# Hybrid decoder layer with a PEER mixer: 24 instead of 16 tokens take their U products from gathered rows, and two of eight heads of the fourth token block are searched later

## The chip, the core and the metric

The kernel runs on one core of a Trainium2 chip, whose engines are named as in the profile: PE (TensorE), DVE (VectorE), ACT (ScalarE), POOL (GpSimd) and SP (SyncE, which here only sets off DMAs). The metric is the device time of one execution in microseconds. Before the change it is 1616.67 us, the median of three runs (1615.92 to 1617.07).

## The reference, cut to what matters

One layer for 512 tokens of width 1024 in float32: a mixer of state-space heads and latent attention (not touched by the change), and then PEER, a lookup among 16384 experts:

```
def block(xb):                                   # 128 tokens at a time
    q = (xb @ w_query).reshape(T, 8, 2, 128)     # 8 heads, two halves
    s = jnp.einsum('thkd,hknd->thkn', q, sub_keys)           # 128 sub-keys a half
    sv, si = lax.top_k(s, 16)                    # best 16 of each half
    cand_s = sv[:, :, 0, :, None] + sv[:, :, 1, None, :]     # 256 candidates a head
    cand_i = si[:, :, 0, :, None] * 128 + si[:, :, 1, None, :]
    top_s, top_pos = lax.top_k(cand_s, 16)       # 16 experts a head
    expert_idx = jnp.take_along_axis(cand_i, top_pos, axis=-1)
    gate = jax.nn.softmax(top_s, axis=-1)
    u = jnp.take(u_table, expert_idx, axis=0)    # rows of a 16384 x 1024 table
    act = jax.nn.gelu(jnp.einsum('td,thkd->thk', xb, u), approximate=False)
    v = jnp.take(v_table, expert_idx, axis=0)
    return jnp.einsum('thk,thkd->td', gate * act, v)
```

So each token has 128 pairs of an expert and a gate (8 heads by 16). A residual sum and a layer norm follow.

## The kernel before

**Arithmetic.** Nearly all products are float32 made of three products of a split form: a weight tile `wir` is read from memory, ScalarE rounds it to its high part `wih` (L109), VectorE subtracts to get the low part `wil` (L119), and `mm3` (L71 to L74) multiplies high by high, high by low and low by high. The class `Stream` holds the weights in one fixed order (`item()` gives the next). Fetching an item also has the splits made of the two items behind it and the raw loads of those after, which SP issues; so the low part of a U item is made, in VectorE's order, about two U chunks before TensorE needs it. During the query products the low part is GpSimd's (`lo_on`).

**PEER in two ways.** Blocks 0 to 2 of the tokens (`NT` = 384) are computed against the whole tables: a *U chunk* (`u_half`, L1223) multiplies 128 experts' rows of the U table by the transposed tokens, 8 x 3 matmuls whose moving side is `NU` tokens wide, and a Gelu (L1233) leaves `act`. A *V chunk* (`v_mm`, L1385) multiplies `act` times gate by 128 rows of the V table, 18 matmuls of 512 columns into six banks that are summed over all 128 chunks. The gate times activation is made in `v_prep` (P, L1362), and split by `v_hi` (Ph, ScalarE L1375) and `v_lo` (Pl, VectorE L1382). Block 3 is done by gathering rows: 128 rows of U for its 128 tokens, products on VectorE (L1440), and 128 rows of V (L1446), each by an indirect DMA of GpSimd (L1429, five buffers).

**The last `UG` tokens of block 2** are not in the U chunks (`NU` = `NT` - `UG`). For each of them its 128 expert rows are gathered (`ug_index` L1057, `ug_fetch` L1069, three buffers `urow`), multiplied by the token's row spread over the partitions (`ux`) and summed by one VectorE instruction (`ug_dots`, L1078). Those activations are multiplied into the gate (`ug_head`, L1088), and the chunks' `act` is filled with ones there (L1232), with a scale per token.

**Stages around the change** (us in the profile of before):

- 423 to 549: query products `w_query_fm`, sub-key scores, and the search on VectorE. `top16` (L947) runs max, max_index, match_replace, max, max_index for each of the four token blocks; `stage1` (L964) does so for both halves of a head and then for 88 sums that hold its best 16.
- 549 to 593: `stage2` (L1037) decodes the indices of blocks 0 to 2; those of block 3 are stored to memory and decoded much later (`late3`, L1044).
- 595 to 770: the *build*. `build_g` (L1126) makes the gate matrix, 128 x 128 experts for every token of blocks 0 to 2, in 48 groups of eight tokens. `hot` makes two one-hot tiles on VectorE (ij L1134, g L1139), one group ahead; TensorE does 16 small float16 matmuls (L1157, L1158); ScalarE copies them to `stg` (L1160); every fourth group its queue stores them in two parts (gs0 L1164, gsp L1165). From group 1 on, one product of `ug_dots` follows each group.
- 770 to 790: the rest of the first `LEAD` = 54 U chunks and, behind the first gate loads (`load_g`, L1333, issued by SP, L1337), the first V chunk.
- 790 to 1382: one U chunk and one V chunk in turns. The gather of block 3 is mixed in by `gather` (L1407), which begins with `late3`.
- 1382 to 1606: V chunks alone.

**What sets the order.** The order on each engine is written out. Two clocks of estimated time are kept, `tm[0]` for TensorE and `tm[1]` for VectorE; `drive` (L1278) puts the next half U chunk (`T_U`/2 us) when TensorE's is behind, and else the next piece of the stage's generator, whose `yield` tells its cost. In search, decode and build, U chunks are so put until `LEAD` - `RES` = 52 of them are placed. Each group of the build adds 2.42 us, each product 1.2. In the V stage, `pump` (L1176) takes pieces of `gather` worth 2.1 us for a V chunk and twice that where a U chunk goes with it, until the rows begin; from there the share of the rows that is due is worked out from the units left.

Of the kernel before, what the change touches and what calls it, by code (L numbers as in the profile page):

```python
# [11 lines left out]
F32 = mybir.dt.float32  # L12
# [12 lines left out]
D = 1024  # L25
NB = 4
# [14 lines left out]
ENDU = 15  # L41
# [12 lines left out]
def tile_block(ctx: ExitStack, tc: tile.TileContext, I, out):  # L54
# [11 lines left out]
    def close(*ps):  # L66
        for p in ps:
            opened.remove(p)
            p.release()
# [810 lines left out]
    one = xt.tile([128, UG], F32, name="one")  # L880
    scl = xt.tile([128, 1], F32, name="scl")
    V.memset(one, 1.0)
    V.memset(scl, 1.0)
# [33 lines left out]
            V.tensor_tensor(ol, pv_, oh, op=OP.subtract)  # L917

    sc, qT = {}, {}

    def w_query_fm(m):
        if m < 16:
# [24 lines left out]
    def top16(src, w, val, idx):  # L947
        t2 = []
        for b in range(NB):
            V.max(val[:, b, 0:8], src[:, b])  # L950
        for b in range(NB):
            V.max_index(idx[:, b, 0:8], val[:, b, 0:8], src[:, b])
        for b in range(NB):
            t2.append(rt.tile([128, 128], F32, name="t2", bufs=4)[:, :w])
            V.match_replace(t2[b], val[:, b, 0:8], src[:, b], NEG)  # L955
        for b in range(NB):
            V.max(val[:, b, 8:16], t2[b])
        for b in range(NB):
            V.max_index(idx[:, b, 8:16], val[:, b, 8:16], t2[b])
        return NB * (0.36 + w * 0.0064)  # L960

    IJG = {}

    def stage1(m):  # L964
        yield top16(sc.pop(m), 128, TV4[:, :, m], TI4[:, :, m])
        if m % 2:
            h = m // 2
            cand = rt.tile([128, NB, 88], F32, name="cand")
            for c0, a0, na, w in ((0, 0, 1, 16), (16, 1, 3, 8), (40, 4, 12, 4)):
                sh = [128, NB, na, w]  # L970
                V.tensor_tensor(cand[:, :, c0:c0 + na * w].rearrange("p h (a b) -> p h a b", a=na),
                                TV4[:, :, m - 1, a0:a0 + na, None].to_broadcast(sh),
                                TV4[:, :, m, None, 0:w].to_broadcast(sh), op=OP.add)
            yield 0.7 + top16(cand, 88, TS4[:, :, h], PO4[:, :, h])

    t3d = [dram.tile([128, n, 16], dt, name=nm) for n, dt, nm in ((8, F32, "ts3"), (8, U32, "po3"), (16, U32, "ti3"))]

    def decode(p, TS, PO, TI, ia, blocks, nb):
        f4 = lambda z: z.rearrange("p b h k -> p (b h k)")
# [56 lines left out]

    def stage2():  # L1037
        for dst, t in zip(t3d, (TS4, PO4, TI4)):
            nc.sync.dma_start(dst, t[:, 3])
        yield from decode(rt2, TS4[:, :3], PO4[:, :3], TI4[:, :3], iaE, (0, 1, 2), 3)  # L1040

    late = []
# [12 lines left out]
    GT, UR = {}, {}  # L1055

    def ug_index(tmp):  # L1057
# [6 lines left out]
        G.dma_start(UR["ix"], bass.AP(tensor=ugi.tensor, offset=ugi.offset, ap=[[UG, 128 // UG], [128, UG], [1, UG]]))  # L1064
        G.dma_start(UR["g"], ugg)
        for n in range(3):
            ug_fetch(n)

    def ug_fetch(n):  # L1069
        if n < UG:  # L1070
            UR[n] = ug.tile([128, D], F32, name="urow", bufs=3)
            G.indirect_dma_start(out=UR[n], out_offset=None, in_=I["u"],
                                 in_offset=bass.IndirectOffsetOnAxis(ap=UR["ix"][:, n:n + 1], axis=0))

    def ug_dots():
        for n in range(UG):
            r = UR.pop(n)
            V.scalar_tensor_tensor(r, r, 1.0, UR["x"], op0=OP.mult, op1=OP.mult, accum_out=UR["hd"][:, n:n + 1])  # L1078
            ug_fetch(n + 3)
            yield 1.2  # L1080
        A.activation(UR["hd"], UR["hd"], AF.Gelu)
        G.dma_start(bass.AP(tensor=ugh.tensor, offset=ugh.offset, ap=[[UG, 128 // UG], [128, UG], [1, UG]]), UR["hd"])
        G.dma_start(UR["w"], ugh)
        close(ug)
        aps.append(pool("act2"))
        yield 0.1
# [39 lines left out]
    def build_g():  # L1126
# [19 lines left out]
        for n in range(48):  # L1146
# [15 lines left out]
            tm[0] += 0.95  # L1162
            if g % 4 == 3:
                nc.scalar.dma_start(gs0[b * 4 + g // 4], stg[:, 0:8])  # L1164
# [58 lines left out]
    def u_half(c, e, psum=None):  # L1223
# [68 lines left out]
    for m in range(17):  # L1292
# [9 lines left out]
        while tm[1] < tm[0] + T_Q:  # L1302
            c = next(fill, None)
            if c is None:
# [4 lines left out]
    close(rq)  # L1309
    ug = pool("ug")  # L1310
    UR["x"] = ug.tile([128, D], F32, name="ux")
    nc.sync.dma_start(UR["x"], bass.AP(tensor=xsp.tensor, offset=xsp.offset + (3 * 128 - UG) * D,
                                       ap=[[0, 128 // UG], [D, UG], [1, D]]))
    UR["ix"] = ijp.tile([128, UG], I32, name="uix")
# [11 lines left out]
    UR["w"] = gb.tile([UG, 128], F32, name="uw")  # L1326
    UR["m"] = gb.tile([UG, 2], F32, name="um")
    drive(build_g(), 1)
    close(gb, *gs)
    vst = pool("vst")  # L1330
    gt = {}

    def load_g(q):  # L1333
        if q < 32 and q not in gt:
            gt[q] = vst.tile([128, NT // 32, 4, 32], F32, name="gt", bufs=2)
            src, q0 = (gs0, q * 4) if q < 2 else (gsp, q * 4 - 8)
            nc.sync.dma_start(gt[q], src[:, :, q0:q0 + 4, :].rearrange("b j i t -> j b i t"))  # L1337

    for q in range(2):
        load_g(q)  # L1340
    if UO:
        step_u()
    uc = un[0]
# [128 lines left out]
    while vc <= LASTC:  # L1472
# [166 lines left out]
```

## Time and profile before

| | |
|---|---|
| median of three runs | 1616.67 us (1615.92 to 1617.07) |
| the profiled execution | 1618.11 us, with a span of 1616.4 us from the first to the last instruction |
| granted TensorE clock | 0.997 on average |
| moved by DMA | 395.42 MB in 152253 packets, 245 GB/s on average |
| 423 to 549 us, search | PE busy 125.8 us, DVE 117.9, 110 GB/s |
| 549 to 595 us, decoding | PE 44.9, DVE 43.8, 171 GB/s |
| 595 to 770 us, build | PE 173.8, DVE 169.1, 269 GB/s |
| 790 to 1382 us, U and V | PE 592.0, DVE 499.3, 340 GB/s |
| 1382 to 1606 us, V alone | PE 224.0, DVE 196.1, 297 GB/s |

Each row of the stages adds up the time in which an engine ran an instruction. Where PE's busy time is the length of the stretch, TensorE never waited there; how dense its matmuls are inside has to be seen in single instructions, since a busy matmul includes its pipeline's length. The rows that matter are shown below with the argument.

### The profile page before, as it was taken

The numbers are of one execution on the slowest core, as the hardware profiler recorded it, in microseconds if no ns is written. First come the engines' busy times: TensorE is split into PE (matmuls) and PEld (weight loads), VectorE is DVE, ScalarE is ACT, GpSimd is POOL, SyncE is SP. The second block draws the span as 40 slices with busy tenths as digits, with TensorE's granted clock in tenths as the row PEclk, the third lists the DMA queues.
The fourth block names the chain that finished last, engine by engine and source line by source line (L and its number), as shares of the span: only waits on it lengthen the run. The fifth ranks groups of instructions, "written<-read, shape, count | busy, mean of one in ns | idle before, by whom it ended". The sixth has DMA issues, their size and how long they took to land.

```text
span 1616.4 us, 23785 instructions
## 1 busy us (share of the span) xinstructions
PE 1581.7 (98%) x8643; PEld 1392.5 (86%) x8643; DVE 1357.5 (84%) x2564; ACT 708.9 (44%) x1231; POOL 479.2 (30%) x340
## 2 busy tenths in 40 slices
PE   6999999999999999999999999999999999999997
PEld 5787878878888999999999999999999999888886
DVE  8979767746799999999488888888888888989987
ACT  5575467732433445556443433333333333333341
POOL 0000010000133223100045555555555555555300
PEclk9999999999999999999999999999999999999999
DMA  6242122364333458877689999999999999999963
GB/s 242 96 156 88 52 77 55 107 234 156 121 91 93 126 173 324 295 250 251 215 293 363 347 357 352 352 346 341 350 351 354 342 346 360 351 336 365 333 226 120
DMA packets 152253, 395.42 MB, mean 245 GB/s; under 512 B 12776, under 2 KB 65720, under 8 KB 150344
## 3 DMA queue, kind: packets, MB, share of 16 engines
q1 hardware_dynamic: 104952, 213.19, 39.6%
q0 software_dynamic: 43584, 155.29, 26.2%
q10 hardware_dynamic: 3600, 25.43, 4.1%
q8 instruction: 68, 1.11, 0.3%
q14 instruction: 49, 0.40, 0.1%
HBM read 359.99 MB, written 31.78 MB: 242 GB/s over the span
## 4 chain that ended last, share of the span: by engine, by line
PE 80%; DVE 14%; ACT 3%; DMA 1%; issue 1%; DVEq 0%; ACTq 0%
PE va L1391 10%; PE va L1395 10%; PE va L1392 10%; PE pu L72 10%; PE pu L74 10%; PE pu L73 10%; PE pa L74 3%; PE pa L73 3%; PE pa L72 3%; DVE t L955 1%; PE pw L73 1%; PE pw L74 1%; PE pw L72 1%; PE pw L1157 1%; DVE wil L119 1%; PE pw L1158 1%
## 5 line engine op out<-in xcount | busy, mean ns | idle before, releaser
L109 ACT ACTIVATE wih<-wir 128x1024 fp32r<-128x1024 f32 (+2 forms) x269 | 278.0, 1034 | 300.2 <-DMA wir<-ut 108.1
L119 DVE TENSOR_TENSOR wil<-wir,wih 128x1024 fp32r<-128x1024 f32 (+1 forms) x254 | 302.0, 1190 | 94.0 <-ACT wih L109 54.8
L74 PE MATMUL pu<-XTH,wil 128*128 128x368 f32 x1008 | 331.8, 329 | 1.0 <-DVE wil L119 0.9
L72 PE MATMUL pu<-XTH,wih 128*128 128x368 f32 x904 | 299.9, 332 | 0.1
L73 PE MATMUL pu<-XTL,wih 128*128 128x368 f32 x904 | 296.8, 328 | 0.0
L1392 PE MATMUL va<-wil,Ph 128*128 128x512 f32 x726 | 282.7, 389 | 0.0
L1429 POOL DMA_INDIRECT row<-u,ix x128 | 191.3, 1494 | 245.1 <-DVE row L1440 122.9
L1429 POOL DMA_INDIRECT row<-v,ix x128 | 189.2, 1478 | 173.1 <-DVE ac L1446 147.8
L74 PEld LDWEIGHTS pu<-XTH,wil 128*128 128x128 f32 x1008 | 189.0, 188 | 1.8 <-DVE wil L119 1.6
L72 PEld LDWEIGHTS pu<-XTH,wih 128*128 128x128 f32 x904 | 169.5, 188 | 3.2 <-ACT act L1233 0.3
L73 PEld LDWEIGHTS pu<-XTL,wih 128*128 128x128 f32 x904 | 169.7, 188 | 2.9
L1391 PE MATMUL va<-wih,Ph 128*128 128x512 f32 x432 | 168.5, 390 | 0.0
L1446 DVE SCALAR_TENSOR_TENSOR ac<-row,hd,ac 128x1024 f32<-128x1024 f32 x128 | 164.1, 1282 | 3.5 <-DMA row<-v,ix 1.3
L1392 PEld LDWEIGHTS va<-wil,Ph 128*128 128x128 f32 x726 | 136.2, 188 | 26.0
L1440 DVE SCALAR_TENSOR_TENSOR row<-row,x 128x1024 f32<-128x1024 f32 x128 | 150.5, 1220 | 4.3 <-DMA row<-u,ix 4.3
L109 ACT ACTIVATE wihx<-wir 128x1024 fp32r<-128x1024 f32 x67 | 71.1, 1061 | 156.8 <-DMA wir<-v 141.5
L1395 PE MATMUL va<-wih,Pl 128*128 128x512 f32 x432 | 133.3, 390 | 0.0
L1233 ACT ACTIVATE act<-pu 128x368 f32<-128x368 f32 x126 | 59.7, 474 | 163.2 <-PE pu L74 163.1
L1391 PE MATMUL va<-wihx,Ph 128*128 128x512 f32 x294 | 114.8, 391 | 0.0
L119 DVE TENSOR_TENSOR wil<-wir,wihx 128x1024 fp32r<-128x1024 f32 x62 | 75.8, 1223 | 41.3 <-issue 29.9
L1395 PEld LDWEIGHTS va<-wih,Pl 128*128 128x128 f32 x432 | 81.2, 188 | 17.2
L1391 PEld LDWEIGHTS va<-wih,Ph 128*128 128x128 f32 x432 | 81.1, 188 | 15.8
(458 smaller groups left out, 3073.4 us busy)
## 6 DMA issues: line engine op xcount, KB each, us to landing
wir<-ut SPq DMA_DIRECT2D x128, 512.0 KB, 5.7
wir<-v SPq DMA_DIRECT2D x128, 512.0 KB, 6.6
gsp<-stg ACTq DMA_DIRECT2D x12, 1920.0 KB, 7.9
gt<-gsp SPq DMA_DIRECT2D x30, 768.0 KB, 10.5
wir<-wo SPq DMA_DIRECT2D x26, 512.0 KB, 3.7
wir<-wf SPq DMA_DIRECT2D x18, 512.0 KB, 3.4
wir<-wqr SPq DMA_DIRECT2D x16, 512.0 KB, 3.7
de<-acd POOLq DMA_DIRECT2D x8, 512.0 KB, 5.1
```

The costliest lines, as they stand in the source:

```text
L72: T.matmul(ps, lh, rh, start=start, stop=False)
L73: T.matmul(ps, lh, rl, start=False, stop=False)
L74: T.matmul(ps, ll, rh, start=False, stop=stop)
L109: A.activation(h, r, AF.Copy)
L119: self.lo(n).tensor_tensor(l, r, h, op=OP.subtract)
L1233: A.activation(ACT[c][:, :NU], ps, AF.Gelu)
L1391: T.matmul(va[b][e], Ph[:, bs], h[:, cs], start=c == 0, stop=False)
L1392: T.matmul(va[b][e], Ph[:, bs], l[:, cs], start=False, stop=False)
L1395: T.matmul(va[b][e], Pl[:, bs], h[:, cs], start=False, stop=c == 127)
L1429: G.indirect_dma_start(out=R[s], out_offset=None, in_=I["u"] if s < 128 else I["v"], in_offset=bass.IndirectOffsetOnAxis(ap=ix[:, s % 128: ...
L1440: V.scalar_tensor_tensor(r, r, 1.0, x3, op0=OP.mult, op1=OP.mult, accum_out=hd[:, s:s + 1])
L1446: V.scalar_tensor_tensor(ac, r, hd[:, s - 128:s - 127], ac, op0=OP.mult, op1=OP.add)
```

## The change

1. `UG` goes from 16 to 24. The U chunks' moving side shrinks from 368 to 360 tokens, and 24 tokens are gathered, in two index tiles of 16 and 8 (`UGS`). Two products follow each group of the build where one did, so that they end at group 13 and not at group 16. The spread token rows hold 16 tokens at a time (each spread over eight partitions); the tile `ux` is loaded again, by GpSimd, ahead of product 16.
2. The search over block 3 leaves out heads 6 and 7 (score tiles 12 to 15, `LM` = 12): ScalarE's queue stores their scores of block 3 to memory (`sc3`), and `late3` reads them back and searches them in the V stage, ahead of block 3's decoding.
3. The last store of the gate (gsp of group 47) is taken from ScalarE's queue and put on SP's, behind the first two gate loads. The gate tiles `gt` get a pool of their own, opened before the build's buffers are closed, so that these loads don't depend on that store.
4. Planner constants: `T_U` from 4.07 to 4.0, and `pump`'s share in front of the rows from 2.1 to 2.2.

The core of the diff:

```diff
-UG = 16
+UG = 24
+LM = 12
+UGS = ((16, 8), (8, 0))
...
-T_U = 4.07
+T_U = 4.0
...
         A.activation(sc[m].rearrange("p a b -> p (a b)"), ps, AF.Copy)
+        if m >= LM:
+            nc.scalar.dma_start(sc3d[:, m - LM], sc[m][:, 3])
...
     def stage1(m):
-        yield top16(sc.pop(m), 128, TV4[:, :, m], TI4[:, :, m])
+        nb = NB if m < LM else 3
+        z = lambda t, k: t[:, :nb, k]
+        yield top16(rt, sc.pop(m)[:, :nb], 128, z(TV4, m), z(TI4, m))
         if m % 2:
...
+            yield head_top(rt, z(TV4, m - 1), z(TV4, m), z(TS4, m // 2), z(PO4, m // 2))
...
     def late3():
...
+        s3 = lt.tile([128, 1, 16 - LM, 128], F32, name="sc3")
+        nc.sync.dma_start(s3[:, 0], sc3d)
         for z, src in zip(t, t3d):
-            nc.sync.dma_start(z[:, 0], src)
+            nc.sync.dma_start(z[:, 0, :src.shape[1]], src)
+        tv = lt.tile([128, 1, 16 - LM, 16], F32, name="tv")
         yield 3.4
+        for m in range(LM, 16):
+            yield top16(lt, s3[:, :, m - LM], 128, tv[:, :, m - LM], t[2][:, :, m])
+            if m % 2:
+                yield head_top(lt, tv[:, :, m - LM - 1], tv[:, :, m - LM], t[0][:, :, m // 2], t[1][:, :, m // 2])
         yield from decode(lt, *t, ia, (3,), 1)
...
+    def ug_x(q, c, o):
+        UR["x"] = ug.tile([128, D], F32, name="ux")
+        q.dma_start(UR["x"], bass.AP(tensor=xsp.tensor, offset=xsp.offset + (3 * 128 - UG + o) * D,
+                                     ap=[[0, 128 // c], [D, c], [1, D]]))
...
     def ug_dots():
         for n in range(UG):
+            if n == 16:
+                ug_x(G, *UGS[1])
+                yield 0.0
+                yield 0.0
             r = UR.pop(n)
...
             if g % 4 == 3:
                 nc.scalar.dma_start(gs0[b * 4 + g // 4], stg[:, 0:8])
-                nc.scalar.dma_start(gsp[b * 4 + g // 4], stg[:, 8:])
+                if n < 47:
+                    nc.scalar.dma_start(gsp[b * 4 + g // 4], stg[:, 8:])
+                else:
+                    GT["last"] = stg
...
             if n >= 1:
-                tm[1] += next(dots, 0.0)
+                for _ in range(2):
+                    tm[1] += next(dots, 0.0)
...
-            A.activation(ACT[c][:, NU:], one, AF.Copy)
+            A.activation(ACT[c][:, NU:], one[:, 0:1].to_broadcast([128, UG]), AF.Copy)
...
     drive(build_g(), 1)
-    close(gb, *gs)
-    vst = pool("vst")
+    close(gb)
+    gtp = pool("gtp")
...
     for q in range(2):
         load_g(q)
+    nc.sync.dma_start(gsp[11], GT.pop("last")[:, 8:])
+    close(*gs)
+    vst = pool("vst")
...
         if GS[0] < 0:
-            more = pump(fill, 2.1 * w)
+            more = pump(fill, 2.2 * w)
```

`head_top` holds the 88 sums and their `top16`, which stood in `stage1`; `top16` runs over as many blocks as its source has. `stage2` stores the indices of heads 0 to 5 of block 3 only.

More of the change, by code (lines that the diff above doesn't have):

```diff
@@ L879, in tile_block @@
     XTL = xt.tile([128, 8, S], F32R, name="XTL")
-    one = xt.tile([128, UG], F32, name="one")
+    one = xt.tile([128, 16], F32, name="one")
     scl = xt.tile([128, 1], F32, name="scl")
@@ L919, in tile_block @@
     sc, qT = {}, {}
+    sc3d = dram.tile([128, 16 - LM, 128], F32, name="sc3")
     def w_query_fm(m):
@@ L945, in sub_scores, with top16 @@
         A.activation(sc[m].rearrange("p a b -> p (a b)"), ps, AF.Copy)
-    def top16(src, w, val, idx):
+        if m >= LM:
+            nc.scalar.dma_start(sc3d[:, m - LM], sc[m][:, 3])
+    def top16(p, src, w, val, idx):
         t2 = []
-        for b in range(NB):
+        bl = range(src.shape[1])
+        for b in bl:
             V.max(val[:, b, 0:8], src[:, b])
-        for b in range(NB):
+        for b in bl:
             V.max_index(idx[:, b, 0:8], val[:, b, 0:8], src[:, b])
-        for b in range(NB):
-            t2.append(rt.tile([128, 128], F32, name="t2", bufs=4)[:, :w])
+        for b in bl:
+            t2.append(p.tile([128, 128], F32, name="t2", bufs=4 if p is rt else 2)[:, :w])
@@ L955, in top16, with head_top @@
             V.match_replace(t2[b], val[:, b, 0:8], src[:, b], NEG)
-        for b in range(NB):
+        for b in bl:
             V.max(val[:, b, 8:16], t2[b])
-        for b in range(NB):
+        for b in bl:
             V.max_index(idx[:, b, 8:16], val[:, b, 8:16], t2[b])
-        return NB * (0.36 + w * 0.0064)
+        return len(bl) * (0.36 + w * 0.0064)
     IJG = {}
+    def head_top(p, v0, v1, val, idx):
+        nb = v0.shape[1]
+        cand = p.tile([128, NB if p is rt else 1, 88], F32, name="cand")[:, :nb]
+        for c0, a0, na, w in ((0, 0, 1, 16), (16, 1, 3, 8), (40, 4, 12, 4)):
+            sh = [128, nb, na, w]
+            V.tensor_tensor(cand[:, :, c0:c0 + na * w].rearrange("p h (a b) -> p h a b", a=na),
+                            v0[:, :, a0:a0 + na, None].to_broadcast(sh),
+                            v1[:, :, None, 0:w].to_broadcast(sh), op=OP.add)
+        return 0.7 + top16(p, cand, 88, val, idx)
@@ L1063, in ug_index @@
         G.dma_start(ugg, f(ijg[128 - UG:, 2]))
[L1064 removed]
+        for j, (c, o) in enumerate(UGS):
+            G.dma_start(UR["ix"][j], ug_ap(ugi, c, o))
         G.dma_start(UR["g"], ugg)
@@ L1311, in tile_block @@
     UR["x"] = ug.tile([128, D], F32, name="ux")
-    nc.sync.dma_start(UR["x"], bass.AP(tensor=xsp.tensor, offset=xsp.offset + (3 * 128 - UG) * D,
-                                       ap=[[0, 128 // UG], [D, UG], [1, D]]))
-    UR["ix"] = ijp.tile([128, UG], I32, name="uix")
+    ug_x(nc.sync, *UGS[0])
+    UR["ix"] = [ijp.tile([128, c], I32, name=f"uix{c}") for c, _ in UGS]
     UR["g"] = ijp.tile([UG, 128], F32, name="ugw")
```

22 lines of the change are left out of this document (9 added, 13 removed).

## The prediction

> **What bounds the kernel now.** I read the page's table of engines first, then busy time by stretch, then single matmuls in the timeline.
>
> ```profile
> PE 1581.7 (98%) x8643; PEld 1392.5 (86%) x8643; DVE 1357.5 (84%) x2564; ACT 708.9 (44%) x1231; POOL 479.2 (30%) x340
> ```
> ```profile
> 595.00:672.00 77.00, 76.75 (x634) 74.14 (x633) 76.40 (x83) 42.32 (x82) 21.84 (x13) 1.00 0.80 296
> ...
> 860.00:1370.00 510.00, 510.00 (x2644) 463.94 (x2643) 434.98 (x563) 192.46 (x318) 276.87 (x190) 1.00 0.97 349
> 1390.00:1500.00 110.00, 110.00 (x487) 91.06 (x487) 100.36 (x118) 40.38 (x54) 59.24 (x36) 1.00 0.99 353
> ```
> The columns are the stretch, its length, busy time of PE, PEld, DVE, ACT, POOL (instructions), clock, DMA share, GB/s. PE is never idle in the last two, so TensorE sets the pace there: 2644 matmuls in 510 us are 63 pairs of a U chunk (24) and a V chunk (18), 8.10 us a pair. In the build (595 to 672) VectorE is as full as TensorE. And the DMA share is 0.97 or more in the V stage. So three things can bind, and the change touches all three.
>
> ```profile
> 869.80 0.33 PE L73 MATMUL pu<-XTL,wih 128*128 128x368 f32 x1
> ...
> 870.97 0.33 PE L74 MATMUL pu<-XTH,wil 128*128 128x368 f32 x1
> ...
> 1449.89 0.39 PE L1391 MATMUL va<-wih,Ph 128*128 128x512 f32 x1
> ...
> 1450.57 0.39 PE L1392 MATMUL va<-wil,Ph 128*128 128x512 f32 x1
> ```
> Seven steps from 869.80 to 870.97 are 0.167 us for 368 columns; three from 1449.89 to 1450.57 are 0.227 us for 512. The difference, 0.060 us for 144 columns, is 0.41 ns a column.
>
> **The change, part by part.**
>
> *Narrower U products.* 368 columns become 360 in 24 matmuls of each of 128 chunks: 8 x 0.41 ns x 24 = 0.08 us a chunk, 10.2 us in all; 4.4 us of it in the 55 chunks ahead of the first V chunk, 5.8 us in the 73 beside V chunks. This is the whole gain; every other part only decides how much of it is kept. The Trainium skill (TensorE: Matmul & The Clock Gate, Back-to-back issue gap) speaks against it: it gives a sustained spacing of 81 ns at 128 columns and 131 ns at 512, which is 0.13 ns a column, and by that the gain would be 3.2 us. The rows above show 227 ns at 512 and the steeper slope, so the sum goes by them.
>
> *Search: two heads of the fourth block leave it.* One search over four blocks, from the chain of waits:
>
> ```profile
> 540.21 0.76 DVE tv L950 x4
> ...
> 543.83 1.05 DVE ti L959 x4
> ```
> 540.21 to 544.88 is 4.67 us, 1.17 a block. Four of them, and two searches over 88 candidates (about 1.1 each with their sums), take 6.9 us from VectorE. In the changed order 15 U chunks stand between the query products and the first gate group (17 before), and one low-part subtraction fewer on VectorE.
>
> ```profile
> 605.30 1.22 DVE L1078 SCALAR_TENSOR_TENSOR urow<-urow,ux 128x1024 f32<-128x1024 f32 x1
> ...
> 606.45 1.22 DVE L119 TENSOR_TENSOR wil<-wir,wih 128x1024 fp32r<-128x1024 f32 x1
> 607.58 1.22 DVE L1134 TENSOR_TENSOR ij<-iotaE,ijT 128x2048 f16<-128x2048 f16 x1
> 608.84 1.22 DVE L1139 TENSOR_TENSOR g<-ij,gT 128x2048 f16<-128x2048 f16 x1
> 609.98 1.22 DVE L1078 SCALAR_TENSOR_TENSOR urow<-urow,ux 128x1024 f32<-128x1024 f32 x1
> ```
> From start to start a product costs 1.15 us, a subtraction 1.13, the one-hot pair 1.26 + 1.14: 4.68 a group. So VectorE comes to the first group 8.0 us earlier, and TensorE 17 x 4.02 - 15 x 3.94 = 9.2 us earlier (4.02 is 24 x 0.167): TensorE waits about **1 us** that it doesn't wait now (0 to 2).
>
> *Two products a group, 24 in all.* 8 x 1.15 = 9.2 us more on VectorE. Between groups 1 and 9 of the changed order stand 11.5 U chunks, 1.44 a group (1.0 in most groups now). A group on TensorE: 1.44 x 3.94 + 1.0 = 6.7 us; on VectorE: 2.40 + 2 x 1.15 + 1.44 x 1.13 = 6.3 us. By busy time it fits. But the rows come through three buffers, filled by GpSimd:
>
> ```profile
> 606.80 1.68 POOL L1072 DMA_INDIRECT urow<-u,uix  x1 [1.86 <-DVE urow L1078]
> ```
> ```profile
> DMA to landing us min/median/max: 4.9/6.6/10.9
> ```
> The product that starts at 605.30 frees its buffer for a gather at 606.80, 1.5 us later, and the row lands 4.9 to 10.9 us behind that. With two products a group, the second takes the row whose gather the first of the group before set off: it is wanted 6.7 + 1.15 = 7.85 us after that product's start, and is there after 6.4 to 12.4, in the median 8.1. So VectorE waits inside the group, with the subtractions of the next U items and the next one-hot pair queued behind it, and TensorE behind those. In the median 0.25 us are missing, which VectorE's spare 0.4 covers; beside a gate store they are not covered.
>
> ```profile
> gsp<-stg ACTq DMA_DIRECT2D x12, 1920.0 KB, 7.9
> ```
> A store goes out every fourth group, three among the twelve with products. With a landing of about 9 us there (my choice, between median and maximum), some 2 us are lost at each, less what spare is left. The second load of the token rows (the tile ux) queues on GpSimd behind a gather, and product 16 waits for it; some 9.4 us of VectorE work stand between, against about 10 for gather, issue and landing: 0.5 us. I take **3.5 us** for this part; the ends are 0 (landing 4.9) and 10 (landing 8.3 throughout, a row shown under the rivals).
>
> *The end of the build.* U chunks ahead of the V stage are capped at 52, and the changed order reaches that at group 45: groups 45, 46 and 47 stand on TensorE with nothing between them. Each needs a one-hot pair (2.40 us) that can begin only when the group two before is off its buffers; TensorE's own part is 0.9 us. Group 46 is prepared behind the last half chunk; for group 47 TensorE waits 2.5 - 0.9 = **1.6 us** (0 to 3). Now a half chunk of 2 us covers it.
>
> *First V chunk; the last store.*
>
> ```profile
> 769.01 0.24 PE L1157 MATMUL pw<-g,ij 128*128 128x128 f16 x1
> ...
> 770.80 0.33 ACTq L1164 DMA_DIRECT2D gs<-stg  x1
> ...
> 775.35 2.02 SPq L1337 DMA_DIRECT2D gt<-gs  x2
> ...
> 783.40 0.55 DVE L1362 TENSOR_TENSOR P<-act,gt 128x384 f32<-128x384 f32 x1
> ...
> 787.58 1.06 ACT L109 ACTIVATE wih<-wir 128x1024 fp32r<-128x1024 f32 x1 [4.89 <-DMA wir<-ut]
> ...
> 789.00 0.51 ACT L1375 ACTIVATE Ph<-P 128x384 fp32r<-128x384 f32 x1
> ...
> 790.00 0.39 PE L1391 MATMUL va<-wihx,Ph 128*128 128x512 f32 x1
> ```
> Now five U chunks (20.1 us) stand between the last group (769.01) and the first V product (790.00), and the chain of store, gate load, P, Ph just fits; Ph even waits behind a split whose load sat on SP behind the gate loads. After, only three chunks remain: 0.9 + 3 x 3.94 = 12.7 us. The chain without that split is 783.40 + 1.1 - 769.01 = 15.5 us, and the moved store takes 1.9 MB out of the way of gs and gt: the gate store's median landing (2.6 us on the page, 4.4 here) and a load without the store beside it should save about 3. The split's load now stands ahead of the gate loads on SP. So about even: **0.3 us** (0 to 3). On SP the store stands ahead of the weights of the second V chunk; 1.9 MB at 350 GB/s are 5.6 us, and they are wanted 8 us after the first, so I add nothing.
>
> *Two heads searched in the V stage.* They come first in the fill, and VectorE runs in order.
>
> ```profile
> 799.74 0.29 DVE L983 TENSOR_TENSOR dd<-ts 128x128 f32<-128x128 f32 x1 [5.27 <-DMA ts<-ts]
> ...
> 801.21 1.22 DVE L119 TENSOR_TENSOR wil<-wir,wih 128x1024 fp32r<-128x1024 f32 x1
> ...
> 802.54 0.39 PE L74 MATMUL pu<-XTH,wil 128*128 128x368 f32 x1
> ```
> VectorE waits 5.27 us for the spilled tile, then a subtraction ends at 802.43 and TensorE reads it at 802.54: no slack. After, the scores are waited for in the same place, and then come 1.5 us of search instead of 1.5 us of decoding: even. But between the next two U chunks the order puts a second half, its candidates, and two more halves, about 6.2 us for dependent instructions on one block, where now 2.0 + 2.2 us of decoding stand. With 3.3 us for subtractions and P parts around it, the low part of that U chunk comes 1.5 us late, and small sums follow: **2 us** (0.5 to 5). The gather then starts later, but by the order it runs at 3.1 rows a pair against 3.0, and ends at the same V chunk.
>
> *Nothing:* four score stores on ScalarE in the search (0.3 us each, ACT 44% busy), one more index load, the constant that fills 24 columns.
>
> **Sum**: -10.2 + 1 + 3.5 + 1.6 + 0.3 + 2 = -1.8 us. The profiled execution took 1618.11 us, 1.4 above the median of 1616.67; a difference of 1.8 on either gives a median of **1614.9 us**.
>
> **Rivals.**
> *A, the rows come in time* and little is lost at the V stage: -10.2 + 1 + 0 + 1.6 + 0 + 0.5 = -7.1, 1609.6 us. For: in the build the median row is only 0.25 us late. Against: three stores, and the tight row at 802.54.
> *B, the gather loop binds* (slower).
>
> ```profile
> row<-u,ix POOLq DMA_INDIRECT x128, 8.3
> ```
> Rows land in 8.3 us where the transfers run at 349 GB/s. Two rows a group raise the build's 296 GB/s towards that. Then the loop alone sets the group: half of 1.5 + 8.3 + 5.2 = 7.5 us (two groups of one product's loop and the rest of a group) against 6.7, 0.8 us in 12 groups and some at the stores: 10 us. -10.2 + 1 + 10 + 1.6 + 0.3 + 2 = +4.7, 1621.4 us. It turns the sign above 5.3 us, a mean landing near 7.4.
> *C, transfers bind the V stage.* If 349 GB/s is all there is, 5.8 us of gain aren't had: -1.8 + 5.8 = +4.0, 1620.7 us. Against: VectorE hardly waits for rows there,
>
> ```profile
> DVE row L1440 <- DMA row<-u,ix: 3.4, 4, 2.0
> ```
> and 353 GB/s were held for 110 us; the pair, 1% shorter with 3% more rows, asks for about 355. The Trainium skill (DMA: Bandwidth & Descriptors, Where 436 GB/s comes from) says that about 358 GB/s bind transfers between HBM and SBUF; by that rule C stays out, barely.
> That the change does not do what it says is excluded by the order: 360 columns, two products a group.
>
> **How the numbers follow.** Forecast 0.38 (1612.5 to 1617.5), A 0.28, B 0.24, C 0.10. A measurement of this kernel tells about 0.2% (3.2 us) from no change. Faster by that (under 1613.4): A and a fifth of the forecast, 0.35. Slower (over 1619.9): most of B, half of C, 0.25. Within: 0.40. The range reaches to A's and B's middle, **1608.5 to 1622**.
>
> **What would show it.** Steps of 0.164 us at 360 columns confirm the gain; 0.167 would sink the forecast. In the changed build, products waiting for DMA rows: 3 to 4 us in total (A: under 1, B: over 8). Groups 45 to 47 about 1.6 us apart from pure TensorE pace; the first V product 12.7 to 13.5 us behind group 47; one U matmul waiting 1 to 2 us for its low part about 20 us later; pairs of 8.02 us from then on (C: 8.1, with VectorE waiting for rows). It is wrong if a wait shows that isn't listed.

## The result and the profile after

The changed kernel takes **1639.19 us** (median of 4 executions, 1638.12 to 1643.82) against 1616.87 us before: a ratio of 1.0141, 95% interval 1.0129 to 1.0153. It is 22 us slower, well above the range of 1608.5 to 1622.

The engine table of the page of the changed kernel:

```profile
span 1636.5 us, 23838 instructions
PE 1577.4 (96%) x8643; PEld 1384.3 (85%) x8643; DVE 1368.3 (84%) x2587; ACT 707.1 (43%) x1231; POOL 507.6 (31%) x350
```

TensorE has less work than before (1577 us against 1582) and a longer span: it waits. Busy time by stretch, cut at the first gate group, the first V matmul and the last U matmul (columns as in the prediction: stretch, length, PE, PEld, DVE, ACT, POOL, clock, DMA share, GB/s):

```profile
586.30:804.00 217.70, 203.88 (x1690) 194.90 (x1690) 187.04 (x194) 113.24 (x220) 37.04 (x26) 0.98 0.74 261
804.00:1399.00 595.00, 584.46 (x3068) 530.36 (x3067) 498.83 (x701) 223.43 (x371) 300.12 (x206) 0.99 0.94 338
1399.00:1626.00 227.00, 225.64 (x992) 185.32 (x990) 201.82 (x272) 80.73 (x110) 101.49 (x59) 1.00 0.86 303
```

Before, these points lay at 595.5, 790.0, 1382 and 1606. So the gate groups start 9.2 us earlier, as predicted for TensorE's part (the 1 us of waiting for VectorE that was to come off it does not show), but the first V matmul comes 14 us later; the stage of U and V chunks is 3 us longer (595 against 592) and the V chunks alone 3 us (227 against 224). That is the 20 us by which the spans differ.

Three views show what TensorE waited for. First, what VectorE waited for in the build, 595 to 700 us (total, times, longest):

```profile
DVE urow L1110 <- DMA urow<-u,uix: 16.5, 5, 6.7
DVE urow L1110 <- DMA ux<-xsp: 2.3, 1, 2.3
```

18.8 us for gathered rows and for the second load of `ux`, where before VectorE never waited for a row. Behind it TensorE waits 11.8 us in the same stretch:

```profile
PE pw L1190 <- DVE g L1172: 6.8, 4, 5.5
PE pu L76 <- DVE wil L121: 5.0, 2, 3.8
```

Second, the same for TensorE from 775 to 880 us, where the first V chunks and the late search lie:

```profile
PE pu L76 <- DVE wil L121: 8.3, 4, 3.2
PE pw L1190 <- DVE g L1172: 1.7, 1, 1.7
```

The 1.7 us are the last gate groups, for which 1.6 was predicted. Third, the granted clock, in two stretches around the second of those waits in the build and in the matmuls there:

```profile
647.00:651.00 4.00, 0.31 (x2) 0.01 (x1) 3.17 (x6) 2.50 (x5) 1.80 (x2) 0.94 0.81 296
651.00:654.00 3.00, 2.94 (x10) 2.90 (x10) 2.97 (x4) 0.00 (x0) 1.42 (x2) 0.51 0.82 264
```
```profile
651.06 0.67 PE L76 MATMUL pu<-XTH,wil 128*128 128x360 f32 x1 [3.75 <-DVE wil L121]
...
652.43 0.50 PE L74 MATMUL pu<-XTH,wih 128*128 128x360 f32 x1
652.73 0.50 PE L75 MATMUL pu<-XTL,wih 128*128 128x360 f32 x1
```

A wait of 3.75 us is followed by about 3 us at half the clock (steps of 0.30 us), so it costs some 1.5 us more than its length. Shorter waits can do it too. With one product a group (an experiment below):

```profile
847.69 0.43 PE L76 MATMUL pu<-XTH,wil 128*128 128x360 f32 x1 [2.58 <-DVE wil L121]
```
```profile
848.50:852.00 3.50, 3.50 (x14) 3.50 (x13) 3.50 (x6) 1.18 (x2) 0.88 (x1) 0.52 0.87 297
```

A wait of 2.58 us was followed by 3.5 us at half the clock there, while one of 2.55 us in the changed kernel (ending at 819.1) was not. The Trainium skill (TensorE: Matmul & The Clock Gate, Part 1: The HAM clock gate) says that the clock halves after an idle window of about 3.4 us and stays so for about as long; the length agrees with these rows, the 3.4 us as a bound for one wait does not. The prediction had no term for the clock.

The gain is there too, and larger than predicted. U matmuls of the changed kernel beside V chunks, and in the build:

```profile
899.82 0.32 PE L75 MATMUL pu<-XTL,wih 128*128 128x360 f32 x1
...
901.58 0.32 PE L74 MATMUL pu<-XTH,wih 128*128 128x360 f32 x1
```
```profile
785.91 0.33 PE L76 MATMUL pu<-XTH,wil 128*128 128x360 f32 x1
...
787.39 0.33 PE L76 MATMUL pu<-XTH,wil 128*128 128x360 f32 x1
```

Eleven steps in the first are 0.160 us each, nine in the second 0.164. The prediction expected 0.164 everywhere; it holds in the build.

### The profile page after: what moved, and what is told of

Read it like the earlier page. It is cut to its first block, busy times and chain, and to the rows that moved or that the text cites. A ratio compares the mean times of both kernels' runs of the same rounds, so it can differ in the third digit from the quotient of the medians.

```text
span 1636.5 us, 23838 instructions
## 1 busy us (share of the span) xinstructions
PE 1577.4 (96%) x8643; PEld 1384.3 (85%) x8643; DVE 1368.3 (84%) x2587; ACT 707.1 (43%) x1231; POOL 507.6 (31%) x350
## 4 chain that ended last, share of the span: by engine, by line
PE 57%; DVE 19%; DMA 9%; issue 8%; ACT 3%; POOL 3%; SPq 0%; DVEq 0%; POOLq 0%; ACTq 0%
PE va L1430 7%; PE va L1434 7%; PE va L1431 7%; PE pu L74 6%; PE pu L76 6%; PE pu L75 6%; DVE wil L121 4%; DMA wir<-v 3%; DMA wir<-ut 3%; PE pa L76 3%; PE pa L75 3%; PE pa L74 3%; POOL row L1468 1%; PE pw L75 1%; DVE t L961 1%
## 5 line engine op out<-in xcount | busy, mean ns | idle before, releaser
L76 PE MATMUL pu<-XTH,wil 128*128 128x360 f32 x1008 | 330.6, 328 | 15.8 <-DVE wil L121 15.7
L74 PE MATMUL pu<-XTH,wih 128*128 128x360 f32 x904 | 297.8, 329 | 0.9 <-ACT wih L111 0.9
L75 PE MATMUL pu<-XTL,wih 128*128 128x360 f32 x904 | 294.8, 326 | 0.0
L1468 POOL DMA_INDIRECT row<-v,ix x128 | 203.6, 1591 | 155.8 <-DVE ac L1485 129.0
L1479 DVE SCALAR_TENSOR_TENSOR row<-row,x 128x1024 f32<-128x1024 f32 x128 | 150.6, 1221 | 18.5 <-DMA row<-u,ix 10.9
L1434 PE MATMUL va<-wihx,Pl 128*128 128x512 f32 x294 | 90.8, 390 | 0.6 <-DVE Pl L1421 0.6
L121 POOL TENSOR_TENSOR wil<-wir,wih 128x1024 fp32r<-128x1024 f32 x14 | 33.6, 2399 | 185.3 <-PE pw L76 181.4
```

The lines of the kernel that those rows point to most:

```text
L74: T.matmul(ps, lh, rh, start=start, stop=False)
L75: T.matmul(ps, lh, rl, start=False, stop=False)
L76: T.matmul(ps, ll, rh, start=False, stop=stop)
L121: self.lo(n).tensor_tensor(l, r, h, op=OP.subtract)
L1434: T.matmul(va[b][e], Pl[:, bs], h[:, cs], start=False, stop=c == 127)
L1468: G.indirect_dma_start(out=R[s], out_offset=None, in_=I["u"] if s < 128 else I["v"], in_offset=bass.IndirectOffsetOnAxis(ap=ix[:, s % 128: ...
```

## Experiments

**The narrowing alone.** The kernel before, with

```diff
+WC = lambda c: 360
...
-            mm3(ps, h[:, k], l[:, k], XTH[:, k, :NU], XTL[:, k, :NU], k == 0, k == 7)
+            w = WC(c)
+            mm3(ps[:, :w], h[:, k], l[:, k], XTH[:, k, :w], XTL[:, k, :w], k == 0, k == 7)
```

> The kernel before, with the U matmuls 360 columns wide and nothing else: the 8 columns more are left out of the computation (the fill of ones covers them), no row is gathered for them. Theory N (the profile after shows a step of 0.160 us at 360 columns against 0.167 at 368, so the narrowing alone is worth 24 x 128 x 0.0067 = 20 us): 1595 to 1599 us. Theory L (0.41 ns a column, as predicted, and the rest of what the profile after shows comes from elsewhere): 1606 to 1607 us. Theory D (the transfers cannot carry a pair of chunks in under about 8.05 us): waits of VectorE or ScalarE for weights show in the V stage and the time stays above 1602 us.

Measured: 1609.58 us, ratio 0.9952 (0.9929 to 0.9974), but its executions reach from 1601.18 to 1613.34, while those of the kernel before lie within 4 us. The profile is of the one at 1601.18, with a span of 1599.4: 17.0 us under the one before. From its first V matmul to its last U matmul:

```profile
784.20:1362.60 578.40, 578.40 (x3067) 526.88 (x3067) 494.62 (x651) 225.82 (x372) 301.12 (x208) 1.00 0.95 346
```

73 pairs without a gap, 7.92 us a pair; before it was 592 us and 8.10. The first V matmul stands at 784.2, 5.8 us earlier, but 1.5 us of that lie ahead of the first U matmul (522.7 against 524.2), where nothing was changed. So in this execution the narrowing takes 4.3 us off the stretch ahead of the first V matmul, as predicted (4.4), and 13 us in the stage of U and V chunks, where 5.8 were predicted; the V chunks alone then take 2.2 us longer (226.6 against 224.4). About 15.5 us are its own, between theories L (10) and N (20, which took the step of 0.160 for the build too). The median lies in neither's range; why most executions don't get the gain is the subject of the run with fewer rows, below.

**Other widths**, in a single execution (1612.80 us):

```diff
+WID = (384, 376, 372, 368, 364, 360, 356, 352, 344, 336, 368, 362, 358, 354, 366, 380)
+WC = lambda c: NU if c < 64 else WID[c // 4 % 16]
```

> The kernel before, in which the U chunks from 64 on are computed at other widths, four chunks each of 384, 376, 372, 368, 364, 360, 356, 352, 344, 336, 368, 362, 358, 354, 366 and 380 columns (columns beyond 368 are computed in vain, those short of it are left out). Theory N (the step goes in whole units of 16 columns, the width plus 24 rounded up: 0.160 at 360, 0.1667 at 368 and 512 at 0.2267 fit this): 0.1667 us for 361 to 376, 0.160 for 345 to 360, 0.153 at 336 and 344, 0.173 at 380 and 384. Theory L (in proportion to the columns): 0.443 ns a column, so 0.1665 at 376, 0.161 at 364, 0.156 at 352, 0.149 at 336.

Three of the widths in its timeline, two matmuls each, six steps apart:

```profile
898.04 0.33 PE L74 MATMUL pu<-XTH,wih 128*128 128x376 f32 x1
...
899.07 0.34 PE L74 MATMUL pu<-XTH,wih 128*128 128x376 f32 x1
...
996.23 0.33 PE L74 MATMUL pu<-XTH,wih 128*128 128x364 f32 x1
...
997.22 0.33 PE L74 MATMUL pu<-XTH,wih 128*128 128x364 f32 x1
...
1028.68 0.32 PE L74 MATMUL pu<-XTH,wih 128*128 128x360 f32 x1
...
1029.64 0.32 PE L74 MATMUL pu<-XTH,wih 128*128 128x360 f32 x1
```

0.172, 0.165 and 0.160 us a step. Averaged over four chunks of a width: 0.1535 and 0.1533 at 336 and 344; 0.161, 0.160, 0.160, 0.163, 0.160 at 352, 354, 356, 358 and 360; 0.164 at 362; 0.1665 at 364, 366 and 368; 0.170, 0.173, 0.171 at 372, 376 and 380; 0.1745 at 384. So it is a staircase, with a tread about every 16 columns up to 368 and less regular above, much as theory N has it (372 and 376 lie above N's place, 358 and 362 between two treads). From 368 to 360 the kernel goes down one whole tread, 0.0065 us for eight columns, 0.8 ns a column, where the slope over 368 to 512 is 0.41.

**One product a group.** The changed kernel with

```diff
-                for _ in range(2):
-                    tm[1] += next(dots, 0.0)
+                tm[1] += next(dots, 0.0)
```

> The changed kernel with one product of gathered rows a group in place of two (24 products, groups 1 to 27). Theory R (the rows' landing is what the build waits for: VectorE stood 18.8 us for rows and for the tile ux, the same work spread over twice the groups has the buffers filled in time): waits for rows under 3 us in the build, no halved clock there, 1639 - 16 = 1619 to 1626 us. Theory W (VectorE's work itself is too much for the build, so the same 24 products cost about the same wherever they stand): 1633 to 1639 us.

Measured: 1617.65 us (1614.40 to 1623.30), ratio to before 1.0005 (0.9994 to 1.0016). This one line is worth 21.5 us. VectorE's longest wait from 595 to 700 us is now

```profile
DVE urow L1110 <- DMA ux<-xsp: 2.0, 1, 2.0
```

Theory R holds, and by more than the waits themselves: with them went the half clock in the build. The same 24 products cost the build little when they stand one in a group: the first V matmul is at 787.1, against 784.2 with 16 products and 360 columns, and 1.3 us of that difference lie ahead of the first U matmul. The line does one thing more: by the planner's clocks about one U chunk then stands between two groups, in place of 1.4, so the 21.5 us are the price of the whole arrangement, not of the rows' waits alone.

**More buffers, or no store beside the rows.** Two ways to tell why the rows were late, both with two products a group:

```diff
-KEEP = 43
+KEEP = 37
...
-        for n in range(3):
+        for n in range(5):
             ug_fetch(n)
...
-            UR[n] = ug.tile([128, D], F32, name="urow", bufs=3)
+            UR[n] = ug.tile([128, D], F32, name="urow", bufs=5)
...
-            ug_fetch(n + 3)
+            ug_fetch(n + 5)
```

> The changed kernel, two products a group, with five buffers for the gathered rows in place of three (room for them from activation tiles that are not yet in use); the order on TensorE, VectorE, ScalarE and SP is the same. Theory R (the loop of one buffer, product, gather, landing, is too long for two products a group): VectorE's waits for rows in the build fall from 16.5 us to under 4, 1639 - 15 = 1621 to 1626 us, somewhat above one product a group. Theory B (the rows land late because the transfers are full beside the gate stores, however early they are asked for): most of the waits stay, 1631 to 1638 us.

```diff
+                if n in (19, 23, 27):
+                    nc.scalar.dma_start(gsp[n // 4 - 4], stg[:, 8:])
-                if n < 47:
+                if 11 < n < 47:
                     nc.scalar.dma_start(gsp[b * 4 + g // 4], stg[:, 8:])
```

> The changed kernel, two products a group through three buffers, in which the three large gate stores (gsp, 1.9 MB each) that fall among the groups with products are set off twelve to sixteen groups later, beside the stores of groups 19, 23 and 27 and from their tiles, so these three parts of the gate hold other tokens' values; bytes and everything else are the same. Theory G (the rows land late because they queue behind a gate store: each of the long waits follows one): VectorE's waits for rows in the build fall from 16.5 us to under 5, 1639 - 13 = 1622 to 1628 us. Theory U (the loop of three buffers is too long for two products a group anywhere): 8 us of waits or more stay, 1630 to 1637 us.

Measured: 1628.90 us (1.0077, 1.0054 to 1.0100) with five buffers, 1624.12 (1.0055, 1.0026 to 1.0083) without the stores. VectorE's waits from 595 to 700 us, five buffers first:

```profile
DVE urow L1110 <- DMA ux<-xsp: 5.6, 1, 5.6
```
```profile
DVE urow L1110 <- DMA ux<-xsp: 4.6, 1, 4.6
DVE urow L1110 <- DMA urow<-u,uix: 4.0, 2, 3.2
```

Five buffers take all the waits for rows away, and taking away the stores does so for three quarters (16.5 to 4.0 us), with three buffers. So these waits need both: a loop with little room, and a store that lengthens it. But with five buffers the time falls between the two ranges, 11 us above one product a group: of the 8.9 us between those two profiled spans, 4.6 lie ahead of the first V matmul (791.7 against 787.1), where `ux` is now waited for 5.6 us, and 4.9 in the stage of U and V chunks. What share the order of the U chunks has in that is open. The first of the long waits can be followed in the changed kernel, on ScalarE's queue, GpSimd and VectorE:

```profile
605.37 0.50 ACTq L1199 DMA_DIRECT2D gsp<-stg  x1
```
```profile
607.10 1.68 POOL L1100 DMA_INDIRECT urow<-u,uix  x1 [2.99 <-DVE urow L1110]
```
```profile
611.42 1.22 DVE L1110 SCALAR_TENSOR_TENSOR urow<-urow,ux 128x1024 f32<-128x1024 f32 x1
...
619.35 1.22 DVE L1110 SCALAR_TENSOR_TENSOR urow<-urow,ux 128x1024 f32<-128x1024 f32 x1 [6.70 <-DMA urow<-u,uix]
```
```profile
605.00:610.00 5.00, 5.00 (x33) 4.99 (x31) 5.00 (x7) 1.75 (x4) 2.60 (x2) 1.00 1.02 310
610.00:615.00 5.00, 5.00 (x42) 4.80 (x40) 2.62 (x4) 2.61 (x5) 2.00 (x2) 1.00 1.03 433
```

The store of 1.9 MB is set off at 605.4, the row for the eighth product at 607.1, and until 619.35, 12.2 us later, the row isn't there, while the DMA engines are full (shares of 1.02 and 1.03). The landing itself is not recorded in this trace; the 12.2 us run to the start of the product that waited for it. The other long waits lie beside the stores at 634.9 and 663.0, but there the late row was set off 0.5 and 1.1 us before the store:

```profile
634.47 1.97 POOL L1100 DMA_INDIRECT urow<-u,uix  x1 [0.30 <-issue]
```
```profile
634.94 0.59 ACTq L1199 DMA_DIRECT2D gsp<-stg  x1
```
```profile
646.58 1.23 DVE L1110 SCALAR_TENSOR_TENSOR urow<-urow,ux 128x1024 f32<-128x1024 f32 x1 [3.15 <-DMA urow<-u,uix]
```

So the row need not stand behind the store to be late: these 12.1 us went by with both on their way. `ux` is a wait of its own: its second load is behind the gather of GpSimd, and the earlier VectorE arrives the longer it stands (2.3, 4.6, 5.6 us).

**The search.** All heads of block 3 up front again, with two products a group and with one:

```diff
-LM = 12
+LM = 16
...
```

> The changed kernel with all eight heads of the fourth block searched up front, as before the change (no spill of scores, nothing searched in the V stage). Theory S (the stalls of TensorE at 816, 827, 845 and 862 us, 9.0 us in all, come of the search standing in VectorE's order there): they go, the start of the build is 1 to 2 us later, 1631 to 1634 us. Theory Q (they come of SP: the moved store and the gate loads make weights and the scores late): most of them stay, 1637 to 1641 us.

> Both together: one product a group, and all heads searched up front. If R and S hold and add: 1639 - 16 - 6 = 1614 to 1620 us. If W and Q hold: 1633 us or more. If R alone holds: as one product a group alone.

Measured: 1633.64 us (1.0111, 1.0087 to 1.0136) and 1618.20 (1.0013, 0.9991 to 1.0035). Against the changed kernel the search up front saves 5.5 us; against the kernel with one product a group it changes nothing (1618.20 and 1617.65). The trace shows both halves of that: the first V matmul comes at 791.5 in place of 787.1, and the U and V stage is 582.8 us long in place of 590.8 (the V chunks alone are 2.8 us longer). So S holds, but in the times the search costs ahead of the V stage about what it costs behind it.

**The late search's loads.** One product a group, and the first piece of `late3` (its five loads) taken ahead of the first V chunk:

```diff
     fill = gather()
+    next(fill)
```

> One product a group, and the loads of the late search (scores, indices) set off on SP before the first V chunk, one pair earlier than in the changed kernel; VectorE's order is the same. Theory S' (the stalls of TensorE at 799, 810, 827 and 845 us of the run with one product a group, 8.2 us in all, begin with VectorE's 4.6 us of waiting for these loads, queued on SP behind weights): stalls under 4 us, 1612 to 1615 us. Theory V (they come of VectorE's work, which is full there with 2.2 us of it a chunk): 1616 to 1619 us, as without.

Measured: 1611.02 us (1607.81 to 1616.73), ratio 0.9960 (0.9945 to 0.9975): **0.4% under the kernel before**, 6.6 us from one line. The line does two things, though, against its expectation: the piece that is taken ahead no longer counts in `pump`, so three more pieces of the search come earlier in VectorE's order. In the changed kernel SP and VectorE show where the loads were late:

```profile
811.57 0.33 SPq L93 DMA_DIRECT2D wir<-ut  x1
...
812.42 0.42 SPq L1062 DMA_DIRECT2D sc<-sc  x1
```
```profile
816.25 0.30 DVE L956 MAX8 tv<-sc 128x8 f32<-128x128 f32 x1 [4.71 <-DMA ts<-ts]
...
863.26 1.23 DVE L1479 SCALAR_TENSOR_TENSOR row<-row,x 128x1024 f32<-128x1024 f32 x1 [7.53 <-DMA x<-xsp]
```

SP issues in order; the scores' load stands behind a weight load that waits for its buffer, and VectorE stands 4.71 us, with the next U chunk's low part behind it. From there VectorE is late, so its buffers come free late, so SP is late, and the load of `x` for the first row (7.53 us) is the same again. TensorE's waits from 770 to 880 us, with one product a group and then with the loads early (the largest of each):

```profile
PE pu L76 <- DVE wil L121: 7.6, 4, 2.6
```
```profile
PE pu L76 <- DVE wil L121: 3.2, 1, 3.2
```

And VectorE's order, with one product a group first:

```profile
798.83 0.29 DVE L956 MAX8 tv<-sc 128x8 f32<-128x128 f32 x1 [4.58 <-DMA po<-po]
...
800.42 1.21 DVE L121 TENSOR_TENSOR wil<-wir,wih 128x1024 fp32r<-128x1024 f32 x1
```
```profile
796.23 0.28 DVE L956 MAX8 tv<-sc 128x8 f32<-128x128 f32 x1
...
802.74 1.21 DVE L121 TENSOR_TENSOR wil<-wir,wih 128x1024 fp32r<-128x1024 f32 x1
```

The wait of 4.6 us for the loads is gone, as theory S' has it (the time lies 1 us under its range), but in that place VectorE now does four pieces of the search ahead of the next low part, where it did one. How the 6.6 us divide between the loads and the order is not separated. What is left, 3.2 us, stands behind those four pieces (6.5 us of search).

**The moved store.** One product a group, and `gsp` of group 47 back on ScalarE's queue:

```diff
-                if n < 47:
-                    nc.scalar.dma_start(gsp[b * 4 + g // 4], stg[:, 8:])
-                else:
-                    GT["last"] = stg
+                nc.scalar.dma_start(gsp[b * 4 + g // 4], stg[:, 8:])
...
-    nc.sync.dma_start(gsp[11], GT.pop("last")[:, 8:])
```

> One product a group, and the last gate store back on ScalarE's queue ahead of the gate loads, as before the change. If the moved store does what the prediction took (some 3 us off the chain to the first V product): 1620 to 1622 us, the first V product 2 to 3 us later behind the last group. If the chain is not what TensorE waits for there: 1616 to 1619 us. If the store on SP holds up the weights and the scores of the V stage: 1612 to 1616 us.

Measured: 1618.33 us (1.0004, 0.9988 to 1.0020), the same as without (1617.65). The first V matmul does wait for its operand then,

```profile
787.19 0.50 PE L1425 MATMUL va<-wihx,Ph 128*128 128x512 f32 x1 [1.95 <-ACT Ph L1409]
```

so the move does save about 2 us there, of the 3 predicted. At the end they can't be seen: the time is in the range given for a chain that TensorE doesn't wait for, but the executions reach from 1613.49 to 1627.15, and the interval is wider than 2 us.

**Fewer rows in the V stage.** The 360-column kernel with three of four gathered rows:

```diff
-            if s < 256:
+            if s < 256 and s % 4 != 3:
                 R[s] = gp2.tile([128, D], F32, name="row", bufs=ROWS)
...
```

> The kernel before with U matmuls of 360 columns (8 columns left out), and of the 256 rows that are gathered for the fourth block every fourth is left out; the instruction that would use it stays, on data that are there, so VectorE's work is the same and the transfers of the V stage are 33 MB (of some 256) less. Theory D (the faster pairs of chunks ask for more than the transfers carry, which spreads the 360-column kernel from 1601 to 1613 us): median 1597 to 1601 us, spread under 3 us. Theory C (the spread has another cause, such as the order of splits): 1605 to 1612 us as with all rows.

Measured: 1600.90 us, all executions between 1600.72 and 1601.81; ratio 0.9901 (0.9887 to 0.9915). The spread of 12 us is gone, and the median is where the fastest execution with all rows was (1601.18). Its U and V stage, and that of an execution at 1627 us (the one profiled with the store back on ScalarE's queue):

```profile
786.60:1365.10 578.50, 578.48 (x3068) 526.90 (x3067) 498.52 (x655) 226.65 (x374) 249.57 (x159) 1.00 0.89 302
```
```profile
787.20:1388.50 601.30, 587.52 (x3066) 528.45 (x3067) 500.47 (x704) 223.62 (x372) 300.46 (x206) 1.00 0.93 332
```

So theory D holds: with all rows, pairs of 7.92 us ask for more than the transfers reliably carry. Two weight loads (1.05 MB), the gate (0.2) and 3.0 rows (1.57) are 2.82 MB a pair, 356 GB/s; in the changed kernel's order it is 3.05 rows and 359. (A slow execution of the 360-column kernel itself was not profiled; the one at 1627 us is the nearest.) Where the changed kernel keeps its pace it carries 356,

```profile
880.00:1200.00 320.00, 320.00 (x1697) 291.43 (x1696) 271.82 (x405) 120.05 (x200) 186.07 (x122) 1.00 0.98 356
1220.00:1320.00 100.00, 97.82 (x505) 88.13 (x504) 86.11 (x87) 36.25 (x61) 51.17 (x39) 0.98 0.95 346
```

and then falls behind; that the lead of its loads is used up by then is likely, but not shown. The Trainium skill (DMA: Bandwidth & Descriptors, Where 436 GB/s comes from) puts the limit of HBM to SBUF at about 358 GB/s. By that rule the prediction kept this case "barely" out, with a demand of 355 that its own terms do not give (see below). The traces come out near it, but not as a ceiling: with one product a group 362 were carried for 200 us, and TensorE never waited.

```profile
1000.00:1200.00 200.00, 200.00 (x1064) 182.46 (x1063) 173.34 (x249) 77.52 (x128) 116.29 (x79) 1.00 0.99 362
```

**Two trials on the best version.** The planner's U time at 4.2, and the rows of block 3 spread to 13 units before the end, each on the version with one product a group and early loads:

```diff
-T_U = 4.0
+T_U = 4.2
```

> One product a group, the late search's loads ahead of the first V chunk, and the planner's U time at 4.2 in place of 4.0, which leaves four U chunks behind the last gate group as the kernel before had (50 are placed by then in place of 52) and half chunks between the last groups. Theory T (the short tail costs the 3.3 us stall of the first U matmul beside V, the 1.7 us between the last two groups and a halved clock): 3 to 5 us less than without, 1606 to 1608 us. Theory P (TensorE loses the same ahead of the tail, since VectorE sets the build's pace): 1609.5 to 1612 us.

```diff
-ENDU = 15
+ENDU = 13
```

> One product a group and early loads for the late search, with the gathered rows of the fourth block spread to 13 units before the end in place of 15: about 1.2% fewer rows a pair. If transfers bind the V stage in the slower runs of that kernel (1608 to 1617 us): a median 1 to 3 us lower and less spread, 1608 to 1610 us; if not, 1611 us as without.

Measured: 1613.13 us (0.9979, 0.9969 to 0.9990) and **1608.17 us** (1606.92 to 1608.64; 0.9942, 0.9925 to 0.9958). The first shows no gain, outside both ranges: in the profiled execution (1623.16 us, the slowest of twelve) TensorE waits 7.3 us from the first gate group into the first V chunk, against 2.2 without, so what the four U chunks behind the last group cover is lost ahead of them. The second is the fastest kernel here that computes everything, 8.7 us under the one before, and its spread is 2 us where it was 9. That the transfers did this is not shown: by VectorE's order it has 3.00 rows a pair in place of 3.02, as many as the 360-column kernel that spread over 12 us, and there are only four executions.

## Why the prediction was wrong

- **The sign came from the two products a group.** The step that failed is "With a landing of about 9 us there (my choice, between median and maximum), some 2 us are lost at each". Beside a store the row took 12.2 us, above the maximum of the trace before (10.9), and at the three stores VectorE lost 6.7, 4.6 and 5.2 us. The term was 3.5 us with ends 0 and 10; taking one product a group shows **21.5**, of which five buffers, which end the waits for rows, take off 10.3. The mechanism was named (the loop of three buffers, the stores, the one-hots and subtractions queued behind), and rival B was this with 10 us, though by a loop that binds in every group, where the runs show waits beside the stores. Two things go with the price: before, a gather was set off every 4.7 us, and the change sets off two within 2 us; and the waits of 3.75 and 5.50 us that TensorE got from it were followed by half the clock. What each is worth was not measured.
- **The gain** was put at 10.2 us by a slope of 0.41 ns a column and measured at **15.5**. "The difference, 0.060 us for 144 columns" was a line through two treads of a staircase. It fits ahead of the V stage (4.3 us for 4.4) and not in it (13 for 5.8). It made the result better, not worse: alone it brings 7.2 us in the median execution (1616.76 to 1609.58). But shorter chunks also cover less of every wait, and ask more of the transfers.
- **Transfers in the V stage** were costed at 0 and, as rival C, given a chance of 0.10. In the kernel with 360 columns alone they take 8.7 us from the median execution (1609.58 against 1600.90). The argument "asks for about 355" is short by its own terms: 349 GB/s times 8.10/8.02, with 3.1 rows a pair for 3.0 (0.05 of 2.83 MB), is 359, against the 353 that were held for 110 us before.
- **The late search** was costed at 2 us, by VectorE's work, and the loads at nothing: "the scores are waited for in the same place ... even" counted the wait as covered because a wait of 5.27 us was covered before, though the row behind it showed no slack. Setting the loads off earlier, with three pieces of the search earlier in VectorE's order, is worth 6.6 us. The work itself came as forecast: with one product a group 6.5 us of search stand between two low parts (803.61 to 810.12), and the U matmul behind them waits 1.5 us.
- **Right**: TensorE's part up to the first gate group (9.2 us earlier; the 1 us of waiting there did not come), the last groups (1.7 against 1.6), the chain to the first V matmul (12.8 us behind the start of group 47, for which 12.7 to 13.5 was given). The second load of `ux` was named as a wait, with 0.5 us for what took 2.3.

By measured terms: -15.5 + 21.5 + 6.6 leaves 7.5 of the 20 us between the profiled spans, for which the 8.7 of the transfers are the nearest price. The terms come from medians and from single profiles, and how much of the transfers' price fell into the one profiled execution is not separated from what the eight products more cost one a group, and from the waits that stay at 800 us.

## What to carry to other kernels

A gather whose result is used in order needs as much lead as its landing beside the largest store it can meet, not beside the median; with its uses spread it cost little here, and doubling their rate cost 21.5 us. When a tightly packed stage is made faster, work out anew what its transfers must carry and which waits lose their cover. Loads for work that comes later belong ahead of the queue in which they would stand behind buffers' waits.

## What the runs showed of the hardware

- In the V stage the step of these float32 matmuls goes down by 0.0065 us at 360 and again at 344 columns, and hardly between; from 368 to 360 one gains 4%, from 360 to 352 nothing.
- The same matmul of 360 columns takes 0.160 us in the V stage and mostly 0.164 in the build; why is open.
- A wait of TensorE of 3.75 us was followed by about 3 us at half clock, one of 2.58 us by 3.5 us; one of 2.55 us was not.
- A gathered row of 0.5 MB took 12.2 us beside a store of 1.9 MB from another queue, whether it was set off 1.7 us behind the store or 0.5 us ahead of it (12.1), against 4.9 to 10.9 before.
- With 346 GB/s on average over the U and V stage (358 from 860 to 1100 us), executions of one kernel spread over 12 us; with 302 GB/s over 1.
